# Last expert layer: chunks of a small expert in turn with chunks of a large one, and another order of the kernel's first loads

## The chip, the cores and the metric

The kernel runs on one core of one Trainium2 chip, as one program. The metric is the device time in microseconds (us). The engines are named as in the profile: PE (TensorE; PEld is its weight load), DVE (VectorE), ACT (ScalarE), POOL (GpSimd), SP (SyncE, which here only issues DMAs). The suffix q ("SPq") is an engine's instruction queue, where DMAs are issued.

## The reference, cut to what matters

The program is two transformer blocks over 256 tokens of width 1024, all in fp32. What the change touches is the start of the first mixer, which projects `x` with `ev_w_in` (1024 rows), convolves 12 blocks of 128 of its columns over time (`ev_conv_w`, `ev_conv_b`), and takes 16 narrow columns of the same matrix (2560 to 2575) as `dt`; and the last stage, a layer of 8 experts with top-2 routing:

```python
h = rms_norm(x, l1_moe_norm_2)                  # 256 x 1024
logits = h @ l1_moe_w_router_2                  # 8 experts, the top 2 of each token
for e in range(8):                              # FF = 3584
    y_e = (silu(h @ w_gate[e]) * (h @ w_up[e])) @ w_down[e]
out = x + sum over e of share[token, e] * y_e
```

Each expert has three matrices of 1024 x 3584 in fp32, 14 MB each and 42 MB together, so the 8 experts read 336 MB.

## The kernel before, in words

The kernel is written out as one program, one stage after the other; a tile framework gives buffers out of rings (a tag with so many buffers, handed out in turn) and adds the waits. So on every engine the order of the work is the order of the code.

**Exact fp32 on PE.** Most products run as three matmuls of rounded halves (`mm3`): a 1 MB `slab` (L276 to L292) is loaded on SP's queue into a `raw` buffer, ACT rounds it to its high half (`nc.scalar.copy`, L288, a CAST of 128x1024, twice per slab), DVE subtracts to get the low half (`tt`, L137, twice per slab), both into `wx` buffers, and PE takes 12 matmuls of 128x512.

**Last expert layer, `moe2`.** The experts are sorted on the chip by their number of tokens; `p` is the place in that order. Places 0 to 4 are "large" (up to 128 tokens, slabs as above). Places 5 to 7 are "small" (up to 64 tokens): their weights are loaded into buffers called `whole` and go straight to PE as fp32 operand, with no cast or subtraction, 8 matmul records per MB. `SEQ = (0, 5, 1, 2, 6, 3, 4, 7)` is the order in which the places are run, each one from its first load to its last before the next begins.

An expert has 7 chunks of 512 hidden columns. A chunk of a large expert is two slabs of gate, then two slabs of up (`up`), with ACT's Silu of the gate (128x512) and DVE's product (`stt`) behind them; a chunk of a small one is two loads of gate and two of up (`up_small`), whose results share one PSUM tile, and behind them the Silu (64x512) and the product. The turn of a chunk (4 transposes and their copies, `turn`, `turn_small`) is put off into the next chunk by the list `later`. Then `down` takes 14 MB more. Ahead of an expert PE gathers its tokens (`gather`: 8 steps, each one put between other matmuls by `some()`), and `columns` takes its scales.

**Buffers.** `whole()` hands out 14 buffers in turn: 5 of tag `raw`, 2 of `more`, 7 of `wx` (`WBUFS`, `more=2`). A slab takes one of the 7 `raw` and `more` buffers, and one `wx` for each half of its split.

**Loads.** All of them are issued on SP's queue in the order of the code. Each expert's index is read into a register on SP first (`values_load`, which appears there as TENSOR_LOAD). A load waits on SP for its buffer; what is behind it on SP waits as well.

**The start.** `even_mixer` loads `conv_w` and `conv_b` as rows and turns them into columns by a transpose on PE (`columns`, its `turn` at L248), loads the narrow `dt_w`, and then streams slabs of `ev_w_in`. Small constants (`small_dma`, L162) go through POOL's queue. Ahead of the first slab PE runs 8 matmuls with no use for their results (`awake`).

Of the kernel before, what the change touches and what calls it, by code (L numbers as in the profile page):

```python
# [27 lines left out]
SEQ = (0, 5, 1, 2, 6, 3, 4, 7)  # L28
# [25 lines left out]
    "moe2": dict(t8=1, t4=0, t2=5, t1=3, t0=4, tz=16, hh=7, hl=7, more=2, beside=1),  # L54
# [15 lines left out]
class Fused:  # L70
# [94 lines left out]
    def constants(self):  # L165
# [51 lines left out]

        def row(ap, n):
            t = self.C([P, n])
            self.small_dma(t, ap.partition_broadcast(P))  # L220
            return t
# [6 lines left out]
        for l in range(2):  # L228
            b = self.C([P, 20])
            self.small_dma(b[:, 0:4], A["moe_b_group"][l].partition_broadcast(P))  # L230
            self.small_dma(b[:, 4:20], A["moe_b_expert"][l].partition_broadcast(P))
            self.rt_b.append(b)
# [37 lines left out]

    def piece(self, name, shape, tag):
        if tag == "more":
            return self.ap.tile(shape, F32, name=self.name(name), tag=tag, bufs=self.bufs[tag])
        return self.wp.tile(shape, F32, name=self.name(name), tag=tag, bufs=WBUFS[tag])

    def slab(self, src, k, n):  # L276
        nc = self.nc
        self.raws += 1
        at = self.raws % (WBUFS["raw"] + self.bufs.get("more", 0))
        raw = self.piece("raw", [P, k, n], "raw" if at < WBUFS["raw"] else "more")  # L280
# [173 lines left out]
    def even_mixer(self, x):  # L454
        nc, A = self.nc, self.A
        w = A["ev_w_in"][0]
        turn = self.columns(nc.sync, (("conv_w", A["ev_conv_w"][0].rearrange("j c -> (j c)")), ("conv_b", A["ev_conv_b"][0])))
        h, l = self.transpose_split(x, 8, early=True)
        self.fences, self.holds = [self.turned] * FH, [self.upper_part] * FH
        dt_w = self.narrow(w[:, 2560:2576], queue=nc.sync)  # L460
# [19 lines left out]
        for c in range(DTC):  # L480
            convolve(c)
        raw = self.T([P, 2, 16])
# [97 lines left out]
        self.columns(nc.gpsimd, (  # L580
# [6 lines left out]
        self.f_w = self.narrow(A["od_w_in"][0][:, 1952:1960])  # L587
# [99 lines left out]
    def columns_of(self, *ws):  # L687
# [3 lines left out]
        for w in ws:  # L691
            self.small_dma(wc[:, :, at:at + w.shape[1]], w.rearrange("(k p) c -> p k c", p=P))
# [527 lines left out]
    def diff_constants(self):  # L1220
# [11 lines left out]
        for n in ("l1_da_q_norm_2", "l1_da_k_norm_2"):  # L1232
            self.qk_gains.append(self.C([P, 64]))
            self.small_dma(self.qk_gains[-1], A[n].partition_broadcast(P))
# [143 lines left out]
    def moe2(self, x, out):  # L1378
# [83 lines left out]
        def up_small(p, c):  # L1462

            ps = self.PS([P, 512], "ms")
            for a in range(2):
                ws = []
                for i in range(2):
                    ws.append(self.whole(4, 512))
                    nc.sync.dma_start(ws[i], source(p, i, 4 * a, 4, 512 * c, 512))
                if a == 1:  # L1470
# [15 lines left out]
        def turn_small(hid, hids):  # L1486
# [3 lines left out]
            hids.append(self.T([P, 4, CAP1], tag="hh"))  # L1490
# [32 lines left out]
        def catch_up():  # L1523
            while later:
# [6 lines left out]
        for at, p in enumerate(SEQ):  # L1531
            hids, small = [], p >= SMALL
            first, final = at == 0, at == E - 1
            after = [q for q in SEQ[at + 1:at + 3] if q < SMALL] if small else SEQ[at + 1:at + 2] if first else []
            ahead = iter([(gather_small if q == SMALL else gather, (q, k)) for q in after for k in range(8)])

            def some():
                for f, args in ahead:
                    f(*args)
                    break  # L1540

            if p:
                known[p] = nc.values_load(ids[0:1, p:p + 1], engines=[mybir.EngineType.SP], min_val=0, max_val=E - 1)
            scol = self.T([P, 1])
            if p:
# [6 lines left out]
            for c in range(FF // 512):  # L1552
                hid = self.T([P, 512])
                if small:
                    ps = up_small(p, c)
                    self.act(hid[64:128], ps[0:64], AF.Silu, scale=scol[0:64])
                    self.stt(hid[64:128], ps[64:128], scol[64:128], hid[64:128], OP.mult, OP.mult)
                    later.append((turn_small, (hid, hids)))
                    if c > 4:
                        some()  # L1560
                else:
                    g = up(p, c, 0)
                    catch_up()
                    self.act(hid, g, AF.Silu, scale=scol)
                    u = up(p, c, 1)
                    middle.append(lambda hid=hid, u=u, scol=scol: self.stt(hid, u, scol, hid, OP.mult, OP.mult))
                    if MID < 0 or c == FF // 512 - 1:
                        middle.pop()()
                    later.append((turn, (hid, hids)))
                if p == 0 and c == 1:  # L1570

                    place, to = self.T([P, 1, E]), self.T([P, E, E])
                    self.ranks(place, count[:, None], 1, E)
                    order_k = self.T([P, E])
                    self.ts(order_k, place[:, 0], 1000.0, None, OP.add)
                    self.tt(to, order_k[:, None, :].to_broadcast([P, E, E]), self.slots_k[:, 0:E, None].to_broadcast([P, E, E]), OP.is_equal)

                    def by_place(v):
                        o, m = self.T([P, 2, E]), self.T([P, 2, E, E])
                        self.tt(m, v[:, :, None, :].to_broadcast([P, 2, E, E]), to[:, None].to_broadcast([P, 2, E, E]), OP.mult)  # L1580
                        nc.vector.tensor_reduce(o, m, AX.X, OP.add)
                        return o

                    which, ids = self.T([P, E]), self.T([P, E], I32)
# [136 lines left out]
```

## Time and profile before

| | |
|---|---|
| time, median of 3 runs | 2045.85 us (2044.55 to 2050.49) |
| profiled execution, own time | 2045.89 us |
| its span | 2044.1 us |
| mean granted clock of PE | 0.989 |
| PE busy | 1961.7 us, 96% of the span |
| DVE, ACT busy | 1198.0 us (59%), 986.4 us (48%) |
| DMA | 576.44 MB, mean 282 GB/s |
| last expert layer, experts in places 5, 1, 2, 6, 3, 4, 7 | 1235.62 to 2035.00 us of the span |

The rows of the windows view give, for a stretch, the busy time of each engine with its number of instructions, then the clock granted to PE (1.00 is full), the busy share of the DMA engines, and GB/s. PE is busy nearly throughout, but its ends are modelled, and a matmul that waits for its operand within a row can be counted as busy; how long one MB takes PE is therefore read from the distance between rows. Idle time ahead of a row stands in brackets with what ended it.

### The profile page before, as it was taken

The page shows a single profiled execution, that of the slowest core. Times are in us where ns is not written, and L with a number is a line of the kernel's source. Part 1 is how long each engine was busy: PE and PEld are TensorE (multiplying, and loading weights), DVE is VectorE, ACT ScalarE, POOL GpSimd, SP SyncE. Part 2 cuts the span into 40 slices and gives each one's busy share as a digit, 9 for nine tenths or more (in the row PEclk, how much of TensorE's full clock was granted, in tenths as well). Part 3 has the DMA queues.
Part 4 walks back from the last instruction along what each step waited for, and adds up shares of the span by engine and source line. Part 5 has one row for each costly group of instructions (what it writes and reads, how often), then busy time and mean ns, then how long its engine had stood idle before and what let it go on. Part 6 is the DMA issues. An engine that isn't in the chain of part 4 may idle for free. (4 is left out here: it accounts for less than half of the span.)

```text
span 2044.1 us, 26905 instructions
## 1 busy us (share of the span) xinstructions
PE 1961.7 (96%) x10164; PEld 1398.0 (68%) x10164; DVE 1198.0 (59%) x1853; ACT 986.4 (48%) x1472; POOL 42.5 (2%) x66
## 2 busy tenths in 40 slices
PE   7999998999989999999999999999999999999987
PEld 6977445865437989997778884377777337777731
DVE  6856215644136656665777981189897018988700
ACT  4564213642135445445565871177676127777510
POOL 2000000000001000000000000000000000000000
PEclk8999998999999999999999999999999999999999
DMA  9337896547996455554435999999999999999998
GB/s 265 120 119 248 301 368 217 181 147 255 366 347 204 157 165 173 180 185 147 164 124 185 354 341 386 403 386 382 360 348 365 387 402 387 375 353 352 372 387 325
DMA packets 327410, 576.44 MB, mean 282 GB/s; under 512 B 11738, under 2 KB 124088, under 8 KB 327144
## 3 DMA queue, kind: packets, MB, share of 16 engines
q1 hardware_dynamic: 324808, 568.33, 79.2%
q0 software_dynamic: 2464, 6.31, 1.1%
q8 instruction: 82, 1.34, 0.3%
q14 instruction: 56, 0.46, 0.1%
HBM read 573.55 MB, written 1.05 MB: 281 GB/s over the span
## 5 line engine op out<-in xcount | busy, mean ns | idle before, releaser
L137 DVE TENSOR_TENSOR wx<-raw,wx 128x1024 fp32r<-128x1024 f32 (+3 forms) x642 | 749.8, 1208 | 167.8 <-ACT wx L288 164.3
L288 ACT CAST wx<-raw 128x1024 fp32r<-128x1024 f32 (+3 forms) x642 | 636.1, 1042 | 185.6 <-PE acc L149 148.1
L149 PE MATMUL ms<-wx,hl 128*128 128x512 f32 x1960 | 513.6, 396 | 6.5 <-ACT wx L288 2.4
L149 PEld LDWEIGHTS ms<-wx,hl 128*128 128x128 f32 x1960 | 364.2, 189 | 95.7 <-DVE wx L137 15.0
L149 PE MATMUL acc<-hl,wx 128*128 128x256 f32 x2112 | 273.0, 288 | 4.5 <-ACT wx L288 3.4
L149 PEld LDWEIGHTS acc<-hl,wx 128*128 128x128 f32 x2112 | 261.2, 193 | 7.5 <-ACT wx L288 3.9
L134 ACT ACTIVATE t<-ms,tz 128x512 f32<-128x512 f32 (+4 forms) x101 | 60.6, 602 | 281.0 <-PE ms L149 271.8
L149 PE MATMUL acc<-wx,hl 128*128 128x512 f32 (+1 forms) x720 | 181.9, 405 | 4.8 <-DVE wx L137 3.1
L146 DVE SCALAR_TENSOR_TENSOR t<-ms,tz,t 128x512 f32<-128x512 f32 (+2 forms) x69 | 51.7, 749 | 223.8 <-ACT t L134 186.3
L149 PE MATMUL ms<-wx,hh 128*128 128x512 f32 x560 | 179.2, 400 | 1.4 <-DVE wx L137 1.4
L149 PE MATMUL ms<-whole,xg 128*64 128x512 f32 x672 | 165.8, 598 | 12.5 <-DMA whole<-in_l_moe_w_up_dram 12.2
L149 PE MATMUL acc<-wx,t 128*128 128x512 f32 (+1 forms) x732 | 174.1, 394 | 0.5 <-DVE t L1052 0.5
L149 PEld LDWEIGHTS acc<-wx,hl 128*128 128x128 f32 x720 | 136.1, 194 | 36.6 <-DVE wx L137 3.6
L149 PEld LDWEIGHTS acc<-wx,t 128*128 128x128 f32 x732 | 135.3, 188 | 29.9 <-DVE t L1052 0.9
L149 PEld LDWEIGHTS ms<-wx,hh 128*128 128x128 f32 x560 | 104.9, 188 | 28.4 <-DVE wx L137 4.3
L149 PEld LDWEIGHTS ms<-whole,xg 128*64 128x64 f32 x672 | 50.2, 136 | 108.0 <-issue 77.2
L149 PE MATMUL ms<-whole,hl 128*64 128x512 f32 x512 | 117.0, 598 | 0.5 <-DVE t L137 0.5
L149 PE MATMUL ms<-whole,hh 128*64 128x512 f32 x336 | 81.8, 604 | 7.2 <-DMA whole<-in_l_moe_w_down_dram 7.2
L146 DVE SCALAR_TENSOR_TENSOR t<-tp,tz,t 128x512 fp32r<-128x512 f32 x32 | 23.9, 747 | 95.7 <-ACT t L134 95.7
L149 PEld LDWEIGHTS ms<-whole,hl 128*64 128x64 f32 x512 | 35.0, 136 | 59.9 <-issue 55.2
L134 ACT ACTIVATE hl<-tp,c 128x128 fp32r<-128x128 f32 x84 | 29.7, 366 | 85.7 <-PE tp L149 59.5
L146 DVE SCALAR_TENSOR_TENSOR hl<-tp,c,hl 128x128 fp32r<-128x128 f32 x84 | 28.3, 348 | 66.1 <-ACT hl L134 65.4
(282 smaller groups left out, 1578.9 us busy)
## 6 DMA issues: line engine op xcount, KB each, us to landing
raw<-in_l_moe_w_gate_dram SPq DMA_DIRECT2D x70, 1024.0 KB, 7.9
raw<-in_l_moe_w_up_dram SPq DMA_DIRECT2D x70, 1024.0 KB, 8.2
raw<-in_l_moe_w_down_dram SPq DMA_DIRECT2D x70, 1024.0 KB, 7.8
whole<-in_l_moe_w_gate_dram SPq DMA_DIRECT2D x42, 1024.0 KB, 14.0
whole<-in_l_moe_w_up_dram SPq DMA_DIRECT2D x42, 1024.0 KB, 14.0
whole<-in_l_moe_w_down_dram SPq DMA_DIRECT2D x42, 1024.0 KB, 18.3
whole<-in_moe_w_gate_dram SPq DMA_DIRECT2D x64, 512.0 KB, 8.8
whole<-in_moe_w_up_dram SPq DMA_DIRECT2D x64, 512.0 KB, 8.8
```

What stands on the lines that cost most here:

```text
L134: return self.nc.scalar.activation(out, in_, func, **kw)
L137: return self.nc.vector.tensor_tensor(out, a, b, op=op)
L146: return self.nc.vector.scalar_tensor_tensor(out, a, s, b, op0=op0, op1=op1, **kw)
L149: return self.nc.tensor.matmul(out, lhsT, rhs, start=start, stop=stop, **kw)
L288: nc.scalar.copy(h, raw[:, a:a + m])
```

## The change

The last expert layer runs a small and a large expert together: `SEQ` becomes `((0,), (5, 1), (2,), (6, 3), (7, 4))`. In a pair the first two chunks of the small expert come first, with the 8 gathers of the large one, 4 behind each; then chunks of the large (L) and of the small (S) in turn. In full: S0 S1 L0 S2 L1 S3 L2 S4 L3 S5 L4 S6 L5, the small one's `down`, L6, and the large one's `down`. Buffers change: loads of a small expert go in turn to a `wx` buffer and to a `raw` or `more` one (`alternate`), so that gate goes to the ring of `raw` and up to that of `wx`; `more` has one buffer instead of 2, and the small expert's turned chunks have a tag of their own (`hs`, 7 buffers).

At the start, `conv_w` and `conv_b` are loaded on ACT's queue, the narrow `dt_w` and the short constant rows come behind the first two slabs, on SP's queue; other narrow columns (router, `f_w`, norms) go from POOL's queue to SP's at the places where the code stands.

```diff
-SEQ = (0, 5, 1, 2, 6, 3, 4, 7)
+SEQ = ((0,), (5, 1), (2,), (6, 3), (7, 4))
...
-    "moe2": dict(t8=1, t4=0, t2=5, t1=3, t0=4, tz=16, hh=7, hl=7, more=2, beside=1),
+    "moe2": dict(t8=1, t4=0, t2=5, t1=3, t0=4, tz=16, hh=7, hl=7, hs=7, more=1, beside=1),
...
         def row(ap, n):
             t = self.C([P, n])
-            self.small_dma(t, ap.partition_broadcast(P))
+            nc.sync.dma_start(t, ap.partition_broadcast(P))
...
+    def alternate(self, *shape):
+
+        self.wholes += 1
+        return self.piece("whole", [P, *shape], "wx" if self.wholes % 2 else self.raw_tag())
+
+    def raw_tag(self):
+        self.raws += 1
+        return "raw" if self.raws % (WBUFS["raw"] + self.bufs.get("more", 0)) < WBUFS["raw"] else "more"
...
-        turn = self.columns(nc.sync, (("conv_w", A["ev_conv_w"][0].rearrange("j c -> (j c)")), ("conv_b", A["ev_conv_b"][0])))
+        turn = self.columns(nc.scalar, (("conv_w", A["ev_conv_w"][0].rearrange("j c -> (j c)")), ("conv_b", A["ev_conv_b"][0])))
...
-        dt_w = self.narrow(w[:, 2560:2576], queue=nc.sync)
...
+            if c == 1:
+                dt_w = self.narrow(w[:, 2560:2576], queue=nc.sync)
+                self.constant_rows()
...
-                    ws.append(self.whole(4, 512))
+                    ws.append(self.alternate(4, 512))
                     nc.sync.dma_start(ws[i], source(p, i, 4 * a, 4, 512 * c, 512))
+                while middle:
+                    middle.pop(0)()
                 if a == 1:
                     catch_up()
...
+        def chunk(p, c):
+
+            scol, hids = state[p][0], state[p][3]
+            hid = self.T([P, 512])
+            if p >= SMALL:
+                ps = up_small(p, c)
+                self.act(hid[64:128], ps[0:64], AF.Silu, scale=scol[0:64])
+                self.stt(hid[64:128], ps[64:128], scol[64:128], hid[64:128], OP.mult, OP.mult)
+                later.append((turn_small, (hid, hids)))
+                return
+            g = up(p, c, 0)
+            catch_up()
+            self.act(hid, g, AF.Silu, scale=scol)
+            u = up(p, c, 1)
+            middle.append(lambda hid=hid, u=u, scol=scol: self.stt(hid, u, scol, hid, OP.mult, OP.mult))
...
+            few, p = group
+            begin(few)
+            some = ahead(p)
+            for c in range(2):
+                chunk(few, c)
+                some(4)
+            begin(p)
+            for c in range(n - 1):
+                chunk(p, c)
+                if c + 2 < n:
+                    chunk(few, c + 2)
+            down_small(few, ahead(*[q[0] for q in SEQ[at + 1:at + 2] if len(q) == 1]))
+            chunk(p, n - 1)
+            down(p, ahead())
```

What the order of instructions shows at three places. First ACT, among the chunks of the first small expert (place 5), before: `t` out of `ms` with 64x512 is the Silu of one small chunk, `hh` the copy of the turned chunk.

```order
L134 ACTIVATE t_1916_11017<-ms_11018,tz_10976 64x512
L1491 COPY hh_11075<-tp_11070 128x256
L134 ACTIVATE t_1924_11052<-ms_11053,tz_10976 64x512
L1491 COPY hh_11110<-tp_11105 128x256
L134 ACTIVATE t_1932_11087<-ms_11088,tz_10976 64x512
L1491 COPY hh_11145<-tp_11140 128x256
L134 ACTIVATE t_1940_11122<-ms_11123,tz_10976 64x512
```

No cast of a slab stands among them. ACT after, from the end of a chunk of place 5 (the Silu of 64x512) through a chunk of place 1 (CASTs of `raw` into `wx`, two per slab, and the Silu of 128x512):

```order
L135 ACTIVATE t_1954_11203<-ms_11204,tz_10966 64x512
L300 CAST wx_11245<-raw_11243 128x1024
L300 CAST wx_11248<-raw_11243 128x1024
L300 CAST wx_11265<-raw_11263 128x1024
L300 CAST wx_11268<-raw_11263 128x1024
L300 CAST wx_11294<-raw_11292 128x1024
L300 CAST wx_11297<-raw_11292 128x1024
L135 ACTIVATE t_1963_11241<-ms_11242,tz_11093 128x512
L1507 COPY hs_11288<-tp_11283 128x256
L300 CAST wx_11314<-raw_11312 128x1024
L300 CAST wx_11317<-raw_11312 128x1024
```

The four casts of the large chunk's gate slabs now stand behind the Silu of the small chunk that comes before it, and so on at each change from a small chunk to a large one.

Second, SP where the loads of place 5 begin, before, behind the last slab of place 0's `down` (`raw`). TENSOR_LOAD and ISA read the expert's index and work out addresses.

```order
L281 DMA raw_10942<-in_l_moe_w_down_dram 128x4x512
L1543 TENSOR_LOAD tz_10104
L1543 ISA x2
L1469 ISA
L1469 DMA whole_10987<-in_l_moe_w_gate_dram 128x4x512
L1469 ISA
L1469 DMA whole_10989<-in_l_moe_w_up_dram 128x4x512
L1469 ISA
L1469 DMA whole_10999<-in_l_moe_w_gate_dram 128x4x512
L1469 ISA
L1469 DMA whole_11001<-in_l_moe_w_up_dram 128x4x512
```

SP after, at the same place:

```order
L293 DMA raw_10942<-in_l_moe_w_down_dram 128x4x512
L1565 TENSOR_LOAD tz_10104
L1565 ISA x2
L1483 ISA
L1483 DMA whole_10987<-in_l_moe_w_gate_dram 128x4x512
...
L1565 TENSOR_LOAD tz_10104
L1565 ISA x2
L1483 ISA
L1483 DMA whole_10989<-in_l_moe_w_up_dram 128x4x512
L1483 ISA
L1483 DMA whole_10999<-in_l_moe_w_gate_dram 128x4x512
```

Between the first and the second load there are now five reads of an index; and the second load, an up, takes a `wx` buffer, of the ring in which the split halves of place 0's last slabs lie, where before the first loads went to `raw` and `more`.

Third, SP at the start of the kernel, before (`c` out of `in_ev_w_in` is `dt_w`, `raw` the 1 MB slabs, `t` the rows of `conv_w` and `conv_b`):

```order
L82 DMA x_70<-in_x_dram 128x1024 x2
L663 DMA c_182<-in_ev_w_in_dram 128x8x16
L281 DMA raw_196<-in_ev_w_in_dram 128x8x256
L281 DMA raw_264<-in_ev_w_in_dram 128x8x256
L240 DMA t_29_147<-in_ev_conv_w_dram 48x128
L240 DMA t_29_147<-in_ev_conv_b_dram 12x128
L281 DMA raw_329<-in_ev_w_in_dram 128x8x256
L281 DMA raw_477<-in_ev_w_in_dram 128x8x256
```

SP at the start, after:

```order
L83 DMA x_70<-in_x_dram 128x1024 x2
L293 DMA raw_179<-in_ev_w_in_dram 128x8x256
L293 DMA raw_247<-in_ev_w_in_dram 128x8x256
L677 DMA c_312<-in_ev_w_in_dram 128x8x16
L225 DMA c_315<-in_ev_dt_bias_dram 128x16
...
L225 DMA c_321<-in_od_f_bias_dram 128x8
L235 DMA c_323<-in_moe_b_group_dram 128x4
L236 DMA c_323<-in_moe_b_expert_dram 128x16
...
L293 DMA raw_329<-in_ev_w_in_dram 128x8x256
L293 DMA raw_477<-in_ev_w_in_dram 128x8x256
```

The two slabs moved ahead of `dt_w`, the rows of `conv_w` and `conv_b` left this queue, and nine short loads stand between the second slab and the third.

## Rows read from the trace of the kernel before

**Rows 1.** Windows view of core 0, one stretch per expert: places 5, 1, 2, 6, 3, 4, 7.

```profile
1235.62:1331.53 95.91, 94.05 (x436) 34.38 (x434) 11.54 (x25) 14.18 (x32) 0.00 (x0) 1.00 1.04 395
1331.53:1458.37 126.84, 124.22 (x549) 98.52 (x548) 109.00 (x104) 91.78 (x104) 0.00 (x0) 1.00 1.04 381
1458.37:1582.76 124.39, 123.63 (x544) 98.39 (x542) 106.30 (x101) 87.63 (x99) 0.00 (x0) 1.00 1.00 354
1582.76:1683.72 100.96, 96.19 (x435) 35.50 (x434) 11.54 (x25) 14.17 (x32) 0.00 (x0) 1.00 1.04 395
1683.72:1811.97 128.25, 125.62 (x549) 99.69 (x548) 108.99 (x104) 91.67 (x104) 0.00 (x0) 0.99 1.04 380
1811.97:1936.40 124.43, 123.66 (x543) 98.39 (x542) 106.29 (x101) 87.62 (x99) 0.00 (x0) 1.00 1.00 355
1936.40:2035.00 98.60, 85.50 (x371) 27.02 (x369) 6.28 (x10) 8.34 (x17) 0.00 (x0) 1.00 1.00 380
```

**Rows 2.** Timeline of SP: starts of loads, a large expert (L281), then a small one (L1469, L1620).

```profile
1385.41 2.64 SPq L281 DMA_DIRECT2D raw<-in_l_moe_w_gate_dram  x2
...
1397.14 37.29 SPq L281 DMA_DIRECT2D raw<-in_l_moe_w_down_dram  x14
1436.33 0.37 SPq L281 DMA_DIRECT2D raw<-in_l_moe_w_gate_dram  x1
...
1578.98 2.16 SPq L1469 DMA_DIRECT2D whole<-in_l_moe_w_gate_dram  x1
...
1632.65 8.40 SPq L1620 DMA_DIRECT2D whole<-in_l_moe_w_down_dram  x5
```

**Rows 3.** Timeline of PE in place 5: two chunks, then its `down` with a gather.

```profile
1240.60 7.09 PE L149 MATMUL ms<-whole,xg 128*64 128x512 f32 x32
...
1248.01 7.09 PE L149 MATMUL ms<-whole,xg 128*64 128x512 f32 x32
...
1323.53 0.71 PE L149 MATMUL tp<-t,x 128*128 128x128 f32 x4
1324.17 1.94 PE L149 MATMUL ms<-whole,hh 128*64 128x512 f32 x8
1326.04 0.71 PE L149 MATMUL tp<-t,x 128*128 128x128 f32 x4
```

**Rows 4.** Timeline of all engines: a Silu within place 5, then place 5 to place 1.

```profile
1284.79 0.68 ACT L134 ACTIVATE t<-ms,tz 64x512 f32<-64x512 f32 x1 [4.66 <-PE ms L149]
...
1332.07 1.04 ACT L288 CAST wx<-raw 128x1024 fp32r<-128x1024 f32 x1
...
1333.14 7.11 DVE L137 TENSOR_TENSOR wx<-raw,wx 128x1024 fp32r<-128x1024 f32 x6
...
1333.16 0.49 PE L149 MATMUL ms<-wx,hl 128*128 128x512 f32 x1 [1.21 <-ACT wx L288]
...
1334.42 5.54 PE L149 MATMUL ms<-wx,hl 128*128 128x512 f32 x23 [0.76 <-DVE wx L137]
```

**Rows 5.** Timeline of PE, place 6 to place 3, at the same instruction.

```profile
1686.62 7.14 PE L149 MATMUL ms<-wx,hl 128*128 128x512 f32 x23 [0.76 <-DVE wx L137]
```

**Rows 6.** Windows view, two microseconds inside that row.

```profile
1688.00:1690.00 2.00, 2.00 (x6) 1.52 (x5) 2.00 (x2) 2.00 (x3) 0.00 (x0) 0.50 1.06 390
```

**Rows 7.** Timeline of SP: the second load of place 5, issued ahead of its window.

```profile
1211.41 0.38 SPq L1469 DMA_DIRECT2D whole<-in_l_moe_w_up_dram  x1
```

**Rows 8.** Timeline of ACT and PE at the start of the kernel.

```profile
12.71 1.99 ACT L288 CAST wx<-raw 128x1024 fp32r<-128x1024 f32 x2 [3.42 <-DMA raw<-in_ev_w_in_dram]
...
13.81 0.38 PE L149 MATMUL acc<-hl,wx 128*128 128x256 f32 x1 [3.41 <-ACT wx L288]
...
18.90 0.33 PE L248 MATMUL tp<-c,t 64*128 64x64 f32 x1 [4.71 <-DMA t<-in_ev_conv_b_dram]
```

**Rows 9.** Windows view of the start of the kernel.

```profile
22.00:24.00 2.00, 2.00 (x11) 2.00 (x11) 0.00 (x0) 0.93 (x1) 0.00 (x0) 0.50 1.10 350
28.00:30.00 2.00, 2.00 (x19) 2.00 (x18) 1.81 (x3) 1.39 (x3) 0.00 (x0) 1.00 1.09 347
```

## Prediction on record

> **What bounds the kernel now.** First the page's busy shares: PE 96% of the span, so I ask where PE's time is made of waits or of a slow stream. The windows view by expert [rows 1] answers for the last layer, where the change lies: seven stretches, 799.38 us together (their sum). The reader is to see two kinds. The large experts of places 2 and 4 take 124.39 and 124.43 us with PE busy 99% of it and the DMA engines at 354 to 355 GB/s: PE sets their time. The small ones take 95.91, 100.96 and 98.60 at 380 to 395 GB/s, with hardly any work for DVE and ACT. Whether PE or the loads set those, the busy column can't say, since a matmul that waits inside a row counts as busy; the distances do. On SP's timeline [rows 2] a large chunk of four loads takes 1397.14 - 1385.41 = 11.73, and a large `down` 39.19 (1397.14 to 1436.33). A small expert in steady state issues 20 loads from 1578.98 to 1632.65: 2.68 each, 10.73 a chunk. On PE [rows 3] the same chunk, when its loads lie ready, takes 7.41 from start to start, and one MB of small `down` 1.87 (1324.17 to 1326.04). So a small chunk waits for loads for 3.3 us, while a large chunk leaves DMA 1.0 us unused (four loads at 2.68 are 10.7).
>
> Last, the start [rows 8]: the first matmul of the first slab is at 13.81, then PE waits 4.71 for the rows of `conv_b` and goes on at 18.90, and at 22 to 24 the clock granted is 0.50, with 11 matmuls in 2 us, against 19 at 28 to 30 [rows 9].
>
> The sum is made against the profiled execution, 2045.89 us (span 2044.1 and 1.8 around it), which stands at the median of the runs, 2045.85.
>
> **The start.** It removes two loads ahead of the third slab on SP, moves the rows of `conv_w` and `conv_b` to ACT's queue, and nine short loads to the place behind the second slab. PE need not stop for `conv_b`: 18.90 - 13.81 = 5.1 us. If it doesn't stop, the clock need not fall either; I take 6 us at 11 in place of 19 matmuls, that is 6 x 8/19 = 2.5. Together -7.6. Bounds: ACT now issues two DMAs ahead of its first casts and the third slab waits behind nine short loads, which may give back half (-4); the slabs start earlier, and the cast that waits for the first one at 12.71 [rows 8] by up to 2 (-11 with what follows). The narrow columns that go from POOL's queue to SP's later on stand between slabs whose buffers wait for PE: nothing, below and above within 1 us.
>
> **A step of the pair.** One small and one large chunk in turn. Before, 11.73 + 10.73 = 22.46. After, the loads need 8 x 2.68 = 21.4. PE needs 7.41 + 11.73 = 19.14 and one handoff from the small chunk to the large one. The order on ACT says what this is: the Silu of the small chunk, which waits for PE's last matmul of that chunk, stands ahead of the casts of the large chunk's first slab, and PE has nothing else to do. The trace of before has this handoff only where a small expert ends [rows 4]: the cast starts at 1332.07, PE gets one matmul at 1333.16 (after 1.21 of idle) and the other 23 from 1334.42 (after 0.76, waiting for DVE). From the cast's start that is 2.35, less the 0.24 of the one matmul in it (5.54/23); ahead of it the small Silu of 0.68 and about 0.1 to start it: **2.9 us**. DVE's product lies beside the cast. So a step is 22.0 on PE: 0.4 better than before, and the loads (21.4) fit in it by 0.6. Bounds for the handoff: 2.1, if Silu and cast hid one another; 4.5, if the clock falls too (below). From L to S there is no wait: small chunks need no cast, and the product of the large one is put off.
>
> **A whole pair,** from PE's rows: 7 small chunks 7 x 7.41 = 51.9; 8 gathers 8 x 0.64 = 5.1 (1323.53 to 1324.17 [rows 3]); 7 large chunks 82.1; 7 handoffs 20.3 (L0 to L5, and L6 behind the small `down`, which ends in the same way); small `down` 14 x 1.87 = 26.2; large `down` 39.2; what a large expert has beside its chunks and `down`, 124.39 - 121.30 = 3.1; for the small one's columns and scatter 2 (estimate, between 0 and 3). Sum 229.9; in the first pair 8 gathers of place 2 as well, 235.0. Before, the same work took [rows 1]: 5 and 1, 222.75; 6 and 3, 229.21; 4 and 7, 223.03. So **+12.3, +0.7, +6.9, together +19.9**; place 2 stays at 124.4. The reason that little is won in a step and much lost around it: before, a small expert's `down` and gathers and the first 12 loads of the next ran with full buffers, and the handoff was paid twice in all, not 21 times.
>
> **The loads at the head of a pair.** The second load of place 5 was issued at 1211.41, 24 us before its window [rows 7]. After, it takes a buffer of the `wx` ring of 7, in which the last seven halves of place 0 lie; it waits until PE has used the 11th of 14 slabs, 3 x 2.80 (39.19/14) ahead of the window, at 1227. Everything behind it waits on SP, gates too: DMA stands for nearly 16 us. Seven more loads from 1227 at 2.68 are there by 1249, and PE wants the last of them, for S1, at about 1250: just hidden, by the gathers and S0. I take 0; if each load is 1 us later it costs 2 to 4 a pair. This is also why the lead can't be caught up: the steps leave 0.6 each.
>
> **The clock.** From place 6 to place 3, the same 23 matmuls took 7.14 [rows 5] and not 5.54: the granted clock was 0.50 at 1688 to 1690 [rows 6], half speed, behind the idle pieces of 1.21 and 0.76. So one of two handoffs cost 1.6 more. I take half of 21, 16.8, less the 1.6 in before: **+15.2**. Bounds: 0 (-1.6) and all (+32). The Trainium skill ("TensorE: Matmul & The Clock Gate", section on HAM oscillation) tells of a kernel that waits for each slice of data and is throttled at each one; by that rule the term would be +32 and the time that of the second rival below. Our rows show it in one of two.
>
> **Sum:** -7.6 + 19.9 + 15.2 = +27.5, from 2045.89 to **2073**.
>
> **Rivals.** (1) *The loads stream, faster.* Small and large even out: DMA, which in places 2 and 4 runs at 355 GB/s, then has something to do all the time, and PE waits less for it. All 7 x 42 = 294 loads at 395 GB/s, 1.049 MB each, are 781 us against 799.38: -19, with the start 2019. It decides if a handoff costs PE under 2.3 (then 21.4 of loads set the step), the clock holds and the head of a pair loses nothing; half of it gives 2028, reach 2019 to 2039. For it: DMA rates in [rows 1]. Against: the gain in a step is at best 1.0, and the handoff in [rows 4] is longer than that. Chance 0.15.
> (2) *The clock falls at every handoff:* 2045.89 - 7.6 + 19.9 + 32 = 2090, reach 2084 to 2100. For it [rows 5, 6], and that PE now has only 7 us of small matmuls ahead of each; against, the other handoff in [rows 4]. Chance 0.12.
> (3) *Even.* The handoff costs 2.35, Silu and cast overlapping, the clock holds, and the start pays for the rest: 19.9 - 21 x 0.55 = 8.3, less 7.6 and the 1.6 of the one fall in before: 2045, reach 2040 to 2052. Chance 0.12.
> (4) *The start gives nothing* (-4 or less): the forecast stands 4 higher, within its range. That the chunks don't alternate at all is excluded by the order on ACT and SP.
>
> **How the numbers follow.** Forecast 0.61, its own range 2055 to 2086 (clock falls at a quarter to nearly all, handoff 2.5 to 3.2). Range 2040 to 2096: it leaves out case (1) and the top of (2), 0.18. Differences under about 0.3% (6 us) can't be told from no change here. Faster (below 2039.7): case (1), 0.15. Within 0.3%: case (3) with a little of the forecast's lower end, 0.11. Slower: 0.74.
>
> **What would show it.** PE waiting on ACT `wx` and DVE `wx` behind each small chunk, some 2 us, 21 times; windows of a pair at 230 to 245 us; a step of 22 us; a granted clock of 0.5 behind some of the handoffs; SP waiting some 16 us between the first and second load of place 5; PE continuous from about 13 at full clock. Wrong it would be if the casts of the large chunk began before the small chunk ended, if the small chunks still waited for loads (steps over 22.5), or if pairs came out at 212 to 217, the loads' own time.

## The result, and the profile after

The changed kernel takes 2102.11 us (2101.34 to 2102.67, 4 runs) against 2045.2 of before (4 runs): ratio 1.027, 95% interval 1.0254 to 1.0286, some 57 us slower. The direction was forecast; the size was not: 2073 was predicted, and the time lies above the range (2040 to 2096).

The page of the changed kernel (own time of this execution 2101.73):

```profile
span 2100.0 us, 26819 instructions
...
PE 1985.2 (95%) x10164; PEld 1413.0 (67%) x10164; DVE 1200.6 (57%) x1853; ACT 988.5 (47%) x1472; POOL 27.1 (1%) x42
```

PE's share is 95%, hardly less than before, and tells nothing. Its busy time grew by 23.5 us for the same 10164 instructions: first sign of a lower clock, which is 0.976 on the mean where before it was 0.989.

The windows view, by pair (places 5 and 1, then 2 alone, then 6 and 3, 7 and 4):

```profile
1231.53:1475.09 243.56, 224.63 (x982) 137.17 (x981) 122.42 (x130) 106.29 (x135) 0.00 (x0) 0.96 1.00 369
1475.09:1599.05 123.96, 123.31 (x544) 98.49 (x543) 105.26 (x100) 87.62 (x99) 0.00 (x0) 1.00 0.97 344
1599.05:1844.87 245.82, 222.96 (x950) 135.16 (x949) 117.50 (x120) 102.10 (x125) 0.00 (x0) 0.95 0.97 359
1844.87:2093.20 248.33, 224.37 (x950) 136.18 (x948) 118.66 (x123) 102.19 (x126) 0.00 (x0) 0.95 0.93 343
```

Against [rows 1]: the first pair takes 243.56 where places 5 and 1 took 222.75 (+20.8), place 2 alone 123.96 (-0.4), the second pair 245.82 for 229.21 (+16.6), the third 248.33 for 223.03 (+25.3). Together +62. The clock is 0.95 to 0.96 in the pairs and 1.00 in place 2.

What PE waits for in the whole program, the rows of the last layer:

```profile
PE ms L150 <- ACT wx L300: 33.3, 18, 1.9
PE ms L150 <- DVE wx L138: 14.0, 19, 0.8
...
PE tp L150 <- DVE hl L147: 10.1, 12, 1.0
PE ms L150 <- DMA whole<-in_l_moe_w_down_dram: 7.9, 11, 1.8
```

In the kernel before, place 1 has (and place 3 the same two rows):

```profile
PE ms L149 <- ACT wx L288: 1.2, 1, 1.2
PE ms L149 <- DVE wx L137: 1.1, 2, 0.8
```

The rows give the us in total, the number of waits and the longest. So there are 18 waits for the cast, of 1.72 to 1.94, and 18 of some 0.76 for DVE right behind them, where before the two changes from a small expert to a large one had one of each, of 1.21 and 0.76 [rows 4]. PE's timeline over one step, and the start of the next:

```profile
1267.88 3.65 PE L150 MATMUL ms<-whole,xg 128*64 128x512 f32 x16
1271.46 0.66 PE L1497 MATMUL tp<-c,t 128*128 128x128 f32 x4
1272.05 3.65 PE L150 MATMUL ms<-whole,xg 128*64 128x512 f32 x16
1277.55 0.49 PE L150 MATMUL ms<-wx,hl 128*128 128x512 f32 x1 [1.85 <-ACT wx L300]
1278.81 5.50 PE L150 MATMUL ms<-wx,hl 128*128 128x512 f32 x23 [0.77 <-DVE wx L138]
1284.25 0.46 PE L1505 MATMUL tp<-c,t 64*128 64x64 f32 x4
1284.64 5.77 PE L150 MATMUL ms<-wx,hl 128*128 128x512 f32 x24
...
1300.01 0.50 PE L150 MATMUL ms<-wx,hl 128*128 128x512 f32 x1 [1.85 <-ACT wx L300]
1301.27 7.11 PE L150 MATMUL ms<-wx,hl 128*128 128x512 f32 x23 [0.76 <-DVE wx L138]
...
1869.73 8.19 PE L150 MATMUL ms<-wx,hl 128*128 128x512 f32 x24
```

The small chunk is the rows at 1267.88 to 1272.05 (in its middle the turn of the large one). It ends at 1275.7; the large chunk gets one matmul at 1277.55 and goes on at 1278.81: 3.1 us with 0.24 of work in them, so the handoff costs the 2.9 that [rows 4] had been read to. From 1278.81 to 1301.27 a step takes 22.46. The same 23 matmuls take 5.50 in the first step and 7.11 in the second, so that the next step, to 1325.34, takes 24.07. ACT's timeline at that place:

```profile
1275.75 0.68 ACT L135 ACTIVATE t<-ms,tz 64x512 f32<-64x512 f32 x1 [3.01 <-PE ms L150]
1276.45 3.90 ACT L300 CAST wx<-raw 128x1024 fp32r<-128x1024 f32 x4
```

The Silu of the small chunk comes first and the casts behind it, as the order had shown. And the clock, in two windows of the second step:

```profile
1302.00:1304.00 2.00, 2.00 (x6) 1.61 (x5) 2.00 (x3) 2.00 (x3) 0.00 (x0) 0.50 1.05 388
1306.00:1308.00 2.00, 2.00 (x11) 1.64 (x9) 0.90 (x1) 0.00 (x0) 0.00 (x0) 1.00 0.61 113
```

Half speed behind the gap, full speed again by 1306. On PE's timeline 16 of the 18 handoffs have it (7.06 to 7.15 for the 23 matmuls; the other two 5.50 and 5.52), where [rows 5] had it in one of two. The first large chunk of a pair, behind the gathers, has no wait for a cast; the clock fell there in two pairs of three (the row at 1869.73: 8.19 for 24 matmuls, against 5.71 in the first pair). Together 18 of 21 large chunks.

SP's timeline at the head of the first pair:

```profile
1207.32 0.40 SPq L1483 DMA_DIRECT2D whole<-in_l_moe_w_gate_dram  x1
1223.29 0.38 SPq L1483 DMA_DIRECT2D whole<-in_l_moe_w_up_dram  x1
...
1246.91 0.37 SPq L1483 DMA_DIRECT2D whole<-in_l_moe_w_gate_dram  x1
1259.18 0.37 SPq L1483 DMA_DIRECT2D whole<-in_l_moe_w_up_dram  x1
```

The second load of place 5 waits from 1207.7 to 1223.3, 16 us, as worked out. What wasn't: SP stands again from 1247.3 to 1259.2, for the next up load, which takes a `wx` buffer too.

The start, on ACT and PE:

```profile
11.66 0.47 PE L150 MATMUL acc<-hl,wx 128*128 128x256 f32 x1
...
12.61 0.25 PE L253 MATMUL tp<-c,t 64*128 64x64 f32 x1 [0.48 <-DMA t<-in_ev_conv_b_dram]
...
12.79 17.21 PEld L150 LDWEIGHTS acc<-hl,wx 128*128 128x128 f32 x143
...
20.88 2.00 ACT L300 CAST wx<-raw 128x1024 fp32r<-128x1024 f32 x2 [6.52 <-DMA raw<-in_ev_w_in_dram]
```

The first slab's matmul starts at 11.66 and PE runs on from 12.79 at full clock, where [rows 8] has 13.81 and 18.90. DMA moved next to nothing from 12 to 16 us (7 and 15 GB/s in the windows; the third slab waits behind nine short loads, and its cast starts at 20.88), but two slabs are work enough for that time.

### The profile page after: what moved, and what is told of

Same layout as the page of the kernel before. It is cut to its first block, busy times and chain, and to the rows that moved or that the text cites. A ratio compares the mean times of both kernels' runs of the same rounds, so it can differ in the third digit from the quotient of the medians.

```text
span 2100.0 us, 26819 instructions
## 1 busy us (share of the span) xinstructions
PE 1985.2 (95%) x10164; PEld 1413.0 (67%) x10164; DVE 1200.6 (57%) x1853; ACT 988.5 (47%) x1472; POOL 27.1 (1%) x42
## 4 chain that ended last, share of the span: by engine, by line
PE 56%; DVE 6%; DMA 5%; ACT 2%; issue 2%; SPq 0%; POOL 0%; ACTq 0%; DVEq 0%; POOLq 0%
PE ms L150 35%; PE acc L150 18%; DMA raw<-in_l_moe_w_gate_dram 5%; DVE wx L138 4%; ACT wx L300 2%; PE tp L150 1%; PE tp L1497 1%; DVE t L138 0%; DVE hl L147 0%; DVE t L147 0%; ACT t L135 0%; PE av L150 0%; PE tp L1505 0%; PE tp L346 0%; POOL tz L397 0%
## 5 line engine op out<-in xcount | busy, mean ns | idle before, releaser
L150 PE MATMUL ms<-wx,hl 128*128 128x512 f32 x1960 | 546.8, 414 | 48.4 <-ACT wx L300 33.3
L150 PEld LDWEIGHTS ms<-wx,hl 128*128 128x128 f32 x1960 | 385.0, 199 | 159.2 <-ACT wx L300 49.2
L150 PE MATMUL ms<-whole,xg 128*64 128x512 f32 x672 | 153.5, 598 | 0.0
L150 PEld LDWEIGHTS ms<-whole,xg 128*64 128x64 f32 x672 | 44.5, 136 | 81.7 <-issue 80.8
L323 ACT CAST hh<-tp 128x512 fp32r<-128x512 f32 x35 | 20.4, 584 | 140.1 <-PE tp L1497 140.0
L150 PE MATMUL ms<-whole,hs 128*64 128x512 f32 x336 | 77.5, 600 | 7.9 <-DMA whole<-in_l_moe_w_down_dram 7.9
L138 DVE TENSOR_TENSOR hl<-tp,hh 128x512 fp32r<-128x512 f32 x35 | 24.2, 691 | 74.9 <-ACT hh L323 74.8
```

Source lines behind the costliest of these rows:

```text
L138: return self.nc.vector.tensor_tensor(out, a, b, op=op)
L150: return self.nc.tensor.matmul(out, lhsT, rhs, start=start, stop=stop, **kw)
L323: self.upper_part = self.nc.scalar.copy(h, src)
```

## The experiments

Three theories. **Theory 1:** the order on ACT costs the time: 2.9 us of idle PE at each change from a small to a large chunk, and the clock that falls behind it. **Theory 2:** the loads do, held up by the `wx` ring. **Theory 3:** only the clock. Each run stands beside runs of the kernel before on the same chip. The medians of before are 2045.2 to 2048.26 on these chips, so a difference between two runs from different chips is good to some 3 us.

### The idle time filled: awake_gap

```diff
                 ps = up_small(p, c)
+                if c > 1:
+                    self.awake(self.PS([P, 512], "tp"), 9)
                 self.act(hid[64:128], ps[0:64], AF.Silu, scale=scol[0:64])
...
+            self.awake(self.PS([P, 512], "tp"), 9)
             yh, yl = self.T([P, 512], F32R), self.T([P, 512], F32R)
             self.split(yh, yl, psy, gcol)
             later.append((scatter_small, (p == 0, p == LAST, oht, yh, yl)))
```

> The changed kernel with 9 matmuls of 128x512 in bf16, whose results nothing uses, on PE behind each small chunk from the third on and behind each small down: some 2 us of work in the idle 2.6 us, so that PE waits for the same casts without standing idle. Theory 1 with the clock as a part of its own: the 18 stretches at half clock go or become few, the waits for the casts stay; -26 to -31, about 2073. If the clock falls for another reason than the idle time: 2102. Theory 2 (loads set the pair): within 5 of 2102, since a faster PE would wait for loads.

Measured 2074.42 (2074.05 to 2075.44); ratio to before 1.0131 (1.0114 to 1.0148). PE at the handoff:

```profile
1296.82 3.65 PE L150 MATMUL ms<-whole,xg 128*64 128x512 f32 x16
1300.41 2.12 PE L150 MATMUL tp<-c 128*128 128x512 bf16 x9
1302.32 0.50 PE L150 MATMUL ms<-wx,hl 128*128 128x512 f32 x1
1303.58 5.51 PE L150 MATMUL ms<-wx,hl 128*128 128x512 f32 x23 [0.76 <-DVE wx L138]
```

The 9 added matmuls end where the cast is ready, and the 23 matmuls behind them take 5.51; the clock is 1.00 behind all 18 handoffs. So the idle time brings the falls at the handoffs, and these cost some **27.7 us** of the changed kernel (2102.11 - 2074.42; against casts_first below, which has the changed kernel's waits and ran on the same chip as awake_gap, 26.0). Falls behind the gathers stay: two of the three first large chunks run at half clock here too (7.26 and 8.01 for 24 matmuls). The wait itself stays: a step is still 22.4 (1281.15 to 1303.58). So theory 3 is part of the truth, and theory 2, by which a faster PE would have met the loads (within 5 of 2102), is refuted for this kernel.

### The order on ACT: casts_first, casts_ahead, casts_ahead2

casts_first moves code only: the next large chunk's first slab is written ahead of the small chunk's Silu.

```diff
+        def prepare(p, c, slabs):
+            for a in range(slabs):
+                early[p, c, 0, a] = self.slab(source(p, 0, 4 * a, 4, 512 * c, 512), 4, 512)
...
                 ps = up_small(p, c)
+                if then:
+                    then()
                 self.act(hid[64:128], ps[0:64], AF.Silu, scale=scol[0:64])
...
-                    chunk(few, c + 2)
+                    chunk(few, c + 2, lambda: prepare(p, c + 1, 1))
```

> The changed kernel, but the first slab of the next large chunk is loaded, cast and subtracted ahead of the small chunk's Silu in the code (also ahead of the scaling behind the small down). Same work, same loads in the same order. Theory 1 (the order on ACT at the handoff, with the clock that falls behind it, costs the time): the waits of 1.85 and 0.77 go, the clock holds, a step falls from 24.0 to what the loads allow, 21.4 to 21.8; 15 steps by 2.4 and three last chunks by 4.5 make -50, about 2052. Theory 2 (the loads set the pair, because the up loads wait in the wx ring): the wait only moves to the loads, 2090 or more. Theory 3 (only the clock costs): the step loses the 1.6 alone, about 2073.

Measured 2100.37 (2098.02 to 2104.33): no change to speak of. Its timeline says why (the last row is PE's weight load; the matmul behind it starts at the same time, after 1.85 of idle PE):

```profile
1273.88 0.68 ACT L135 ACTIVATE t<-ms,tz 64x512 f32<-64x512 f32 x1 [3.01 <-PE ms L150]
1274.58 3.89 ACT L300 CAST wx<-raw 128x1024 fp32r<-128x1024 f32 x4
...
1275.68 0.19 PEld L150 LDWEIGHTS ms<-wx,hl 128*128 128x128 f32 x1 [2.73 <-ACT wx L300]
```

The Silu still goes first, with the same 18 waits: in this kernel only PE's order is written out by hand (`manual_schedule` with PE alone), while ACT and DVE get their order from the framework. So this run says nothing on theory 1, and it corrects what was said of the kernel before: the order of the code is not the order on ACT and DVE. casts_ahead holds the order with `issue_after`, on top of the edit of casts_first (and the same for the scaling behind the small `down`); casts_ahead2 does it for both gate slabs:

```diff
-                nc.scalar.copy(h, raw[:, a:a + m])
+                self.cast = nc.scalar.copy(h, raw[:, a:a + m])
...
                 if then:
                     then()
-                self.act(hid[64:128], ps[0:64], AF.Silu, scale=scol[0:64])
-                self.stt(hid[64:128], ps[64:128], scol[64:128], hid[64:128], OP.mult, OP.mult)
+                with self.tc.issue_after(self.cast.ins) if then else nullcontext():
+                    self.act(hid[64:128], ps[0:64], AF.Silu, scale=scol[0:64])
+                with self.tc.issue_after(self.sub.ins) if then else nullcontext():
+                    self.stt(hid[64:128], ps[64:128], scol[64:128], hid[64:128], OP.mult, OP.mult)
```

> The changed kernel with the order held on ACT and DVE: the casts and subtractions of the next large chunk's first slab issue ahead of the small chunk's Silu and product (and ahead of the scaling behind the small down). In the run called casts_first only the code was moved, the scheduler put the Silu back ahead, and the waits of 1.85 and 0.77 stayed, 18 and 19 of them. Theory 1 (handoff and the clock behind it): both waits and the half-clock stretches go. The step falls from 24.1 to the loads' 21.4 to 21.8; 15 steps make -36, three last chunks -13: about 2053. If PE then sets the step (19.6): about 2022. Theory 2 (the loads set the pair already): 2090 or more.

> As casts_ahead, but with both gate slabs (four casts) ahead of the Silu. Theory 1: as casts_ahead, less the 0.2 us a step that PE may wait for the second slab: 0 to -4 against it, unless the loads set the step, then the same. Rival: the Silu is now late, and the turn of the small chunk or PSUM waits for it: +5 or more.

Measured 2064.49 (2063.71 to 2066.72) and 2064.64 (2060.1 to 2067.48): 37.6 us of the changed kernel's time go, the second slab ahead adds nothing. The rows of casts_ahead at a handoff:

```profile
1296.45 1.99 ACT L300 CAST wx<-raw 128x1024 fp32r<-128x1024 f32 x2 [2.98 <-DMA raw<-in_l_moe_w_gate_dram]
...
1297.55 0.19 PEld L150 LDWEIGHTS ms<-wx,hl 128*128 128x128 f32 x1 [1.07 <-ACT wx L300]
...
1298.47 0.68 ACT L135 ACTIVATE t<-ms,tz 64x512 f32<-64x512 f32 x1
1298.81 1.23 PEld L150 LDWEIGHTS ms<-wx,hl 128*128 128x128 f32 x6 [1.07 <-DVE wx L138]
```

The cast no longer waits for the small chunk but for its load (2.98, DMA `raw`): the loads set the step now, 21.7 us from one such row to the next (1298.81 to 1320.56), as the expectation of 21.4 to 21.8 has it; in windows of 2 us from 1296 to 1304 the DMA engines run at 385 to 388 GB/s. The 1.85 is 0.19, and in the steps the clock holds; the 0.76 for DVE, which was expected to go too, stays. The whole came out 11 us above the expected 2053: the last chunk behind the small `down` kept its wait (1.90 to 1.98; the cast waits for its load), and the heads of the pairs were not touched. Theory 1 holds for these 37.6 us, and under it lies the next limit.

### The loads: old_rings, in_sequence, seq_old_rings, after_head_raw, head_raw, gathers_hidden

old_rings sends the small loads of the changed kernel through all buffers in turn, as before:

```diff
-                    ws.append(self.alternate(4, 512))
+                    ws.append(self.whole(4, 512))
...
-                w = self.alternate(2, D)
+                w = self.whole(2, D)
```

> The changed kernel, but the loads of a small expert go through the 13 buffers in turn as they did before (5 raw, 1 more, 7 wx) and not gate to one ring and up to the other. Theory 1: the handoffs stay, so within 8 of 2102. Theory 2: the first loads of a pair are early again, -15 to -30, 2072 to 2087.

Measured 2119.68 (2115.23 to 2126.46): 17 us slower, against both theories. Waits of PE for loads rise from 8 to 21.6 us; for these pairs two rings, one for gate and one for up, are the better choice. in_sequence keeps the changed kernel's start, rings and pairs, but runs the chunks of the two experts one expert after the other, with all gathers in the small one's part:

```diff
-            some = ahead(p)
-            for c in range(2):
-                chunk(few, c)
-                some(4)
-            begin(p)
-            for c in range(n - 1):
-                chunk(p, c)
-                if c + 2 < n:
-                    chunk(few, c + 2)
-            down_small(few, ahead(*[q[0] for q in SEQ[at + 1:at + 2] if len(q) == 1]))
-            chunk(p, n - 1)
+            some = ahead(p, *[q[0] for q in SEQ[at + 1:at + 2] if len(q) == 1])
+            for c in range(n):
+                chunk(few, c)
+                if c > 4:
+                    some()
+            down_small(few, some)
+            begin(p)
+            for c in range(n):
+                chunk(p, c)
```

> The changed kernel, start, rings (gate and up in two rings, one more buffer less, hs) and pairs as they are, but the chunks not in turn: all 7 small chunks, the small down with the gathers in it, then the 7 large chunks and the large down. If the turn-taking costs the time (handoffs, exposed gathers): near the start alone, 2039 to 2048, with one handoff per pair. If the rings or the loads held up at the head of a pair cost it: 2060 or more.

Measured 2070.63 (2069.52 to 2071.66). Not the 2039 to 2048 that stood for the turn-taking as the whole cost: without any turn-taking the new layer is 32 us slower than the old one behind the same start (start_only, below). On SP, and in what PE waits for:

```profile
1208.28 0.40 SPq L1483 DMA_DIRECT2D whole<-in_l_moe_w_gate_dram  x1
1224.24 0.38 SPq L1483 DMA_DIRECT2D whole<-in_l_moe_w_up_dram  x1
```

```profile
PE ms L150 <- DMA whole<-in_l_moe_w_up_dram: 27.6, 29, 1.6
```

The head of the pair is held up by the same 16 us, and PE waits for up loads 29 times in the small chunks; start_only has 15 such waits, 12.2 us. Three runs ask whether the first is the cause of the second:

> in_sequence (2070.6), with the small loads going through the 13 buffers in turn as in the kernel before. If the second load, held up 16 us at the head of each pair by the wx ring (1208.28 to 1224.24), is what makes it 32 us slower than the start alone: 2038 to 2046. If one buffer less, hs or the place of the last small expert cost it: 2060 or more.

> The changed kernel, with the 8 loads of the first two small chunks of a pair all through the raw ring, so that they don't wait for wx. The prediction took the late loads at 0, since S0 and S1 with the gathers hide them and the handoffs set the steps: within 4 of 2102. Rival: the late loads are the missing 14 us of the layer: 2085 to 2092.

> gathers_hidden (2062.4: no handoffs on ACT, gathers of place 4 in a small down) with the same early loads. There the loads set the steps (21.7). If the 16 us at the head of each pair are lost for good: 3 x 6 to 3 x 16 less, 2015 to 2044. If buffers are full soon after anyway (SP stood from 1246.4 to 1260.15 in casts_ahead): within 5 of 2062.

The edit of the last two, on the changed kernel and on gathers_hidden:

```diff
-                    ws.append(self.alternate(4, 512))
+                    ws.append(self.piece("whole", [P, 4, 512], self.raw_tag()) if c < 2 else self.alternate(4, 512))
```

Measured 2064.35 (2063.68 to 2065.32), 2097.87 (2095.08 to 2101.17) and 2055.5 (2052.44 to 2056.68). So the rings are 6 of the 32 us in sequence (with them as before PE still waits 22.3 us for up loads, 25 times); the other 26 lie in what that run shares with the change: one buffer less, `hs`, the last small expert ahead of a large one and not at the end. The traces of seq_old_rings and start_only, taken apart at the starts of `columns` on PE, say where: the third pair (places 7 and 4) takes 240.8 for 224.9, place 6 107.0 for 100.7, all other places together some 6 more (the last place counted up to its last scatter; 2 us of these 28 come back ahead of the layer and behind it). Which of the three causes it, they don't say. In the changed kernel the early loads give 4.2, at the edge of the 4 that was expected and far from the rival's 10 to 17; with the handoffs gone 6.9, which is neither the 18 to 47 of one expectation nor quite the 5 of the other. gathers_hidden is casts_ahead with the gathers of place 4 in the small `down` before:

```diff
-            some = ahead(p)
+            some = ahead(*([] if p in inputs else [p]))
...
-            down_small(few, ahead(*[q[0] for q in SEQ[at + 1:at + 2] if len(q) == 1]), lambda: prepare(p, n - 1, 1))
+            down_small(few, ahead(*[q[-1] for q in SEQ[at + 1:at + 2]]), lambda: prepare(p, n - 1, 1))
```

> casts_ahead, with the gathers of place 4 moved from the first two chunks of the third pair into the small down of the second pair, where PE waits for loads. Base 2064.5. If the gathers at the head of a pair stand on the path: -7 to -10 (the head takes 24.4 with them, two chunks alone 14.8), 2055 to 2058. If the loads limit the pair as a whole: within 3 of 2064.

Measured 2062.44 (2061.47 to 2063.85): 2.1 of the 7 to 10 expected. The loads take back what PE gains.

### The two parts alone: start_only, layer_only, and one step further, start_plus

The diff of start_only is that part of the change's diff that touches `row`, `columns`, `dt_w`, `constant_rows` and the narrow columns; layer_only is the rest. start_plus is start_only with the large expert's first slab cast ahead of the scaling of the small result, at the two old changes:

```diff
                 yh, yl = self.T([P, 512], F32R), self.T([P, 512], F32R)
+                if not final:
+                    q = SEQ[at + 1]
+                    known[q] = nc.values_load(ids[0:1, q:q + 1], engines=[mybir.EngineType.SP], min_val=0, max_val=E - 1)
+                    early[q, 0, 0, 0] = self.slab(source(q, 0, 0, 4, 0, 512), 4, 512)
-                self.split(yh, yl, psy, gcol)
+                with self.tc.issue_after(self.cast.ins) if not final else nullcontext():
+                    self.split(yh, yl, psy, gcol)
```

> The kernel before with the change's start alone: order of the first loads, constant rows behind the second slab, narrow columns from POOL's queue to SP's. The last layer as before. In the changed trace the same point of the program comes 9.1 us earlier at 28 us, 6.3 at 160 us and 4.1 at 1222 us. If that is the start's own worth: 4 to 7 below before, 2038 to 2041. If the later loss of 2.5 us was an accident of the clock: 2037 to 2039.

> The kernel before with the change's last layer alone, the start as before. The start alone measured -8.4 against before on its chip. If the two parts simply add: 2102 + 8 = 2110 (2107 to 2113), +63 to +65 against before. If the layer's clock falls depend on what comes ahead: 2095 to 2120.

> The start alone with the old last layer, and at its two changes from a small to a large expert the large one's first slab cast ahead of the scaling of the small result. Each handoff cost 2 us of idle and one of two 1.6 for the clock: 3 to 6 below the start alone, 2033 to 2036 if that is 2038.7. If the scaling that is now late holds up the next: the same or 2 more.

> The start alone once more, beside the last: 2037 to 2041, -0.4% against before.

start_only: 2038.73 (2037.1 to 2039.71), ratio 0.9957 (0.9941 to 0.9974); again 2038.87 (2038.51 to 2039.03), 0.9961 (0.9947 to 0.9975). This is the fastest kernel here, 0.4% below before. layer_only: 2111.16 (2105.16 to 2114.23), ratio 1.0297 (1.0276 to 1.0317): the parts add. start_plus: 2043.73 (2042.1 to 2050.23), 5 us slower than start_only, where 3 to 6 less or at most 2 more were expected. PE at the first of the two changes, in start_only and then in start_plus:

```profile
1327.62 0.50 PE L149 MATMUL ms<-wx,hl 128*128 128x512 f32 x1 [1.21 <-ACT wx L292]
1328.88 5.52 PE L149 MATMUL ms<-wx,hl 128*128 128x512 f32 x23 [0.76 <-DVE wx L137]
```

```profile
1327.41 0.49 PE L149 MATMUL ms<-wx,hl 128*128 128x512 f32 x1 [2.20 <-ACT wx L292]
1328.67 6.85 PE L149 MATMUL ms<-wx,hl 128*128 128x512 f32 x23 [0.76 <-DVE wx L137]
```

On ACT the slab's casts now begin at 1326.31, behind the cast that `columns` makes of its own result (L1524, at 1326.04), where in start_only the first of them (1326.54) stands ahead of it (1327.59). The wait grows by 1.0, and the clock falls behind it; the second change has the same, 2.20 and 6.87 for 1.21 and 5.54. Together that is 4.7 of the 5 us.

## Why the prediction came out wrong

**The step that failed is the clock's term.** "I take half of 21, 16.8, less the 1.6 in before: +15.2" rested on one fall in two. It was 16 in 18 handoffs, which awake_gap prices at some 27.7 us, and two more falls, some 2.5 us each, behind the gathers, where the prediction had counted a handoff. The rival with a fall at every handoff (2090) had the mechanism; its chance of 0.12 was far too small. Two handoffs were no basis for a half, and they were not the same handoff: in both the idle PE waited 1.21 for the cast, while the 2.9 that the prediction itself worked out, with the Silu of 0.68 ahead of the cast, means a wait of some 1.9. Behind 1.21 and 0.76 the clock fell once in six such places (before, start_only and start_only2 have two each), behind 2.20 and 0.76 in both of start_plus, behind 1.85 and 0.76 in nearly all of the changed kernel's. The wait's length is not the whole story: in old_rings, with waits of 1.84 and more, the 23 matmuls took 5.51 to 5.52, full speed, in 5 of 18 places. What decides in the single case is not shown.

The prediction took the Trainium skill ("TensorE: Matmul & The Clock Gate", section on HAM oscillation) for a rule by which each of these waits brings a fall. The kernel of that section is throttled at each slice by waits for DMA that are longer than the waits here, so that section does not state it for waits like these. The measurement decides: here it fell at 16 handoffs of 18.

**The sum of a pair was mis-sized too,** by 16, of which some 4 are falls of the clock. Without the falls at the handoffs the pairs take, in awake_gap:

```profile
1232.31:1469.36 237.05, 229.16 (x1036) 137.38 (x1034) 122.45 (x130) 106.64 (x135) 0.00 (x0) 0.99 1.01 376
1593.16:1828.40 235.24, 223.30 (x1004) 132.02 (x1002) 117.54 (x120) 102.15 (x125) 0.00 (x0) 1.00 1.02 375
1828.40:2067.00 238.60, 226.06 (x1004) 134.30 (x1002) 118.84 (x123) 102.91 (x126) 0.00 (x0) 0.99 0.97 357
```

That is 14.3, 6.0 and 15.6 above before, 35.9 together and not 19.9; the two falls behind gathers that are left (7.26 and 8.01 for some 5.7) are 3.9 of it. Three places show the rest. The first two chunks with the gathers take 24.35 (1231.53 to 1255.88), where 14.8, 5.1 and some of the 5 for columns were put in: the gathers stand in two rows of four, and the later ones of a row wait for DVE's product (`hl`) out of the PSUM tile of an earlier one:

```profile
1250.79 1.16 PE L150 MATMUL tp<-t,x 128*128 128x128 f32 x8
1252.82 0.71 PE L150 MATMUL tp<-t,x 128*128 128x128 f32 x4 [0.87 <-DVE hl L147]
1254.49 0.71 PE L150 MATMUL tp<-t,x 128*128 128x128 f32 x4 [0.96 <-DVE hl L147]
```

In place 5 before they were put one by one into `down`, and 0.64 was all they cost. These waits are 10.1 us in the changed kernel. A step takes 22.4 and not 22.04 (the small chunk with the large one's turn in it 7.8, not 7.41), 6 us in 15 steps. And the small `down` waits for loads (7.9 us in the row of PE's waits), where 14 x 1.87 had it free of them. The three make 24; the three handoffs that the sum has too many (21 for 18, below) take back 8.7. The 15 left are 3 more than there is to explain; the terms for `columns` and scatter were estimates. Either term alone, put right, would have left the forecast at 2084 (27.7 less the 1.6 in before, for 15.2) or 2089, inside the range; both go past its end.

**What held.** The handoff: 2.9 forecast, 2.9 found, 18 times and not 21 (at L0 the gathers and `columns` stand between, and the casts are done by then), and from ACT's order, as said. Place 2: 124.4 forecast, 123.96. The head's load: held up 16 us; the price of 0 for it in this kernel was 4.2 (after_head_raw). The start: -7.6 forecast; -8.4 and -7.3 alone. That agreement is in part luck: where the last layer begins, start_only is 5.5 us ahead of before (1230.08 for 1235.62) and the changed kernel 4.1 (1231.53); some 1.5 of start_only's gain is the fall of [rows 5], which does not occur in its run. That little can be won in a step also held: with the handoff gone the loads set it at 21.7, and the layer stays 17 us above the old one (head_raw against start_only). So the first rival (2019 to 2039) has no base here: in the old order seven experts already took 799.38 for 294 loads, 2.72 each, against 2.68 with the loads back to back.

**What stays open:** what decides whether the clock falls at a given handoff; and which part of the last 17 us is the buffer taken away, the place of the last small expert, or the tail of each pair. By the starts of `columns` in head_raw and start_only they lie in all three pairs: 8, 8 and 4 us.

## What to carry to other kernels

Where the loads nearly fill a stage, taking turns between work bound by loads and work bound by an engine can win no more than the loads still have to give (here 2.72 us a load against 2.68); and each change from one to the other is a handoff with a price of its own, so count the changes before counting what is balanced. Read that price from the engine whose instruction order puts the wait first (here ACT's Silu ahead of the casts), and check in the order of the built program that a reorder took place. Where a change puts many new waits of PE into a kernel, forecast with the clock's fall at every one of them as well as with none, and do not take the share of falls from one or two waits of another length.

## What the runs showed of the hardware

Gaps of some 1.85 and 0.76 us, with one matmul between them, behind a small chunk or a small `down` and ahead of 23 matmuls of 128x512, brought PE's granted clock to 0.50 in 16 of 18 cases of the changed kernel, for 1.6 us each time, and in all 18 of layer_only (6.95 to 7.15 for the 23, where they are one row); in old_rings at least 5 of 18 kept it. Nine matmuls without use in the first gap, with the second of 0.76 left as it was, kept it at 1.00 in all 18 (awake_gap). At one and the same place, a first gap of 2.20 in place of 1.21 brought the fall in 2 of 2 cases (start_plus), where 1 of 6 had it.
